# Output projection with a weight pool of its own and a two-part sample tile; up-projection weights on another queue

## The chip, the core and the metric

The kernel runs on one core of a Trainium2 chip. A core has a matrix engine (TensorE, PE in the rows, with its weight loads as PEld), three engines for elementwise work (VectorE as DVE, ScalarE as ACT, GpSimd as POOL), a queue engine (SyncE, SP) that here does nothing but issue transfers, and 16 DMA engines. ACT issues transfers too, in the order of its own instructions. Every engine runs its instructions in the order in which they were written down for it. The metric is device microseconds from the start to the end of one execution, as a median over executions.

## What is computed

One layer step for 1024 prompt tokens and 64 sample tokens, in float32. A normalised input goes through one input projection; its columns feed 8 heads of differential attention (A) and 16 heads of RWKV-7 time mixing (B); both outputs are gated, put side by side and sent through one output projection, whose normalised result is added to the input. Cut to what matters:

```python
h = rms_norm(x, norm_pre)
proj = h @ w_in
y_a = diff_attention(proj[q, k, v]) * silu(proj[g_a])
m = ps + (prev - ps) * mu_shift                  # token shift, ps = the B columns of proj
w_log = -softplus(-(w0 + tanh(wd) @ w_up)) - 0.5 # wd, ad: 64 columns of m each
a = sigmoid(a0 + ad @ a_up)
y_b = wkv_scan(r, exp(-exp(w_log)), k, v, a)     # then group norm, bonus, gate
mix = concat([y_a, y_b])                         # 2048 wide
out = mix @ w_out                                # 2048 x 1024
x_new = x + rms_norm(out, norm_post)
```

The outputs are x_new for prompt and sample, the keys and values, the final WKV states and the last shifted rows.

## The kernel before

**One program, several streams.** Python generators stand for streams of work. A planner (`Weave`) holds them by rank, keeps a clock of its own, and lets the stream of lowest rank that is ready write down its next instructions; a `yield` gives the modelled time after which a stream may go on, or a condition that it waits for. Streams of high rank are therefore filler: they go on where all others wait. A scheduler then sets each engine's order from this, with the semaphores and the waits for buffers. A pool hands out its tiles by tag, with `bufs` buffers for each tag; a tile that has no free buffer makes the instruction wait that writes it.

**Split operands.** A float32 operand is used as two parts of a format that TensorE takes: `hi` is a copy (ACT, L157) and `lo` the difference (POOL, L158). A product of two split operands takes three matmuls, hi x hi, lo x hi and hi x lo, added up in PSUM.

**Phase B** (`phase_b`) holds 17 units of the RWKV part (8 pairs of heads, two halves of the prompt each, and one unit for the sample, next to last, `p is None`). A unit begins with the up-projections (`w_up`, `a_up`): 64 x 128 weights of one pair, loaded twice, into both halves of a tile of pool tag `t` (5 buffers of 512 columns, `t512`), then split. `load_up` (L513) issues four transfers by ACT's queue (L519), one unit ahead by `next_up` in the unit before; the sample's unit loads four pairs, does their split and matmuls (L550 to L561), and then the other four, in place. Behind that come elementwise work, an inverse in six steps, and a chain over 8 chunks of 64 tokens (`sd` L869, `cbank` L862 to L890, `suv` L900). Filler is `filler` (rank 100): input projections by jobs of 128 columns (L226 to L228), with weights loaded by SP (L165) into a tile that the split of an earlier job has to free (L174).

**Phase A** (`phase_a`) holds the attention, 8 heads of 9 query tiles: `prep` loads a head's queries and keys by SP (`qa`, `ka`) and splits them, `score` and `qtile` do the scores (L1414, L1415), the softmax, and the product with the values (L1475); after four tiles they are turned (L1499) and stored to a DRAM tile `mixd`. Filler is what the projections have left, and then `out_projection`, which is entered when all projections are through and `hctx`, the memory of the projections, is closed; its pool `op` takes that memory.

**The output projection** goes over 7 groups of weights. Groups 0 to 5 are four 128-row blocks of `w_out` by one half (512 columns) of the output; the last has four blocks and both halves. Each group goes over 9 tiles of tokens, `tt` 0 to 7 for the prompt and 8 for the sample's 64. `load_wo` loads and splits a group's weights, into slots 0 to 3, 4 to 7 or 8 to 11, one group ahead; `load_mix` loads four blocks of `mixd` for a tile by SP (L1178) and splits them, for the sample after a memset of the whole tile (L1176), since 64 of its columns have no token. A job then takes for each block three matmuls of 512 columns into PSUM (`po`, two buffers, L1236 to L1238), and adds them to `part[tt]` on DVE (L1247), or copies them there on ACT in groups 0 and 2. In the last group `half_done` squares each half on ACT (L1206), and `finish` scales it by the norm, adds x and stores it (L1213 to L1225); for tiles 3 and 8 a quarter of that is done by POOL. The last group's order is 4, 5, 6, 7, 0, 1, 2, 3, 8, as the last head's query tiles come in the order 7 down to 0, and 8 behind them.

Of the kernel before, what the change touches and what calls it, by code (L numbers as in the profile page):

```python
# [11 lines left out]
F32 = mybir.dt.float32  # L12
# [293 lines left out]
def phase_b(tc, I, O, E):  # L306
# [8 lines left out]
    with ExitStack() as bs:  # L315
# [206 lines left out]
        def unit(n, p, hf):  # L522
# [19 lines left out]
            ups = [nxt.pop()] if nxt else []  # L542
            pss2 = yield from ps512(f"up{u}", 2)
            for q0 in range(0, 8, 4) if smp else (0,):
                if smp:
                    ups = [load_up(q) for q in range(q0, q0 + 4)]
                    yield W_DMA
                for i, raw in enumerate(ups):
                    ups[i] = t = t512(dt=F32R, nm=f"wus{u}{q0 + i}").rearrange("p (s c) -> p s c", c=P)
                    nc.scalar.copy(t[:, 0:2], raw[:, 0:2])  # L550
                    op_(ACT, 256)
                    gtt(t[:, 2:4], raw[:, 0:2], t[:, 0:2].bitcast(F32), op=SUB)
                    d = op_(POOL, 256)
                yield d
                for q, t in enumerate(ups):
                    for j, x in enumerate((xw, xa)):
                        o_ = pss2[j][:, (q0 + q) * CH:(q0 + q + 1) * CH] if smp else pss2[j]
                        cl = slice(TP, T) if smp else slice(hf * HALF, (hf + 1) * HALF)

                        mm(o_, t[:, j], x[:, cl], start=True, stop=False)  # L560
                        mm(o_, t[:, 2 + j], x[:, cl], start=False, stop=True)  # L561
# [487 lines left out]
        def filler():  # L1049
# [46 lines left out]
            yield lambda: len(roped) == 4 and b_done[0]  # L1096
# [18 lines left out]
def out_projection(tc, I, O, E):  # L1115
# [24 lines left out]
    jobs = [(g, tt) for g in range(7) for tt in ((4, 5, 6, 7, 0, 1, 2, 3, 8) if g == LAST else range(9))]  # L1140
# [436 lines left out]
```

## Time and profile before

| | us |
|---|---|
| median of 3 executions | 1816.07 |
| lowest, highest | 1812.95, 1818.63 |
| the profiled execution | 1819.35 |
| its span, first to last instruction | 1817.6 |
| PE busy in the span | 1678.9 |
| DVE, ACT, POOL busy | 1248.0, 846.4, 716.0 |

The profile is one execution. An engine's busy time counts its computing instructions and not the issue of transfers, so an ACT that issues looks idle. A row of a timeline gives start, duration, engine, line, operation and tiles; in brackets stands the idle time before it and what ended that. The granted clock of TensorE has two levels, 1.2 and 2.4 GHz; a stretch gives its mean as a share of the higher one. The row of a stretch gives, after its length, the busy time and in brackets the instructions of PE, PEld, DVE, ACT and POOL in this order.

### The profile page before, as it was taken

Reading aid. Unit: us, or ns where it says so; the run is one execution under the profiler, and the core shown is the slowest. Engines: PE = TensorE matmul, PEld = TensorE weight load, DVE = VectorE, ACT = ScalarE, POOL = GpSimd, SP = SyncE. Lnnn points to the kernel's source line nnn. Section 1 sums busy time; section 2 is a strip of 40 time slices with the busy share of each in tenths; the row PEclk is TensorE's granted clock in tenths of the full one; section 3 lists DMA queues with packets and bytes.
Section 4 is the critical chain, followed back from the end, with each engine's and each line's share of the span. In section 5 each row is a group of like instructions: output and inputs, shape, how many; then the busy total and the mean of one; then the engine's idle time right before and its main releaser. Section 6 shows DMA issues by size and latency. Waiting matters only on the chain.

```text
span 1817.6 us, 34309 instructions
## 1 busy us (share of the span) xinstructions
PE 1678.9 (92%) x12930; PEld 1500.6 (83%) x12930; DVE 1248.0 (69%) x2606; ACT 846.4 (47%) x2027; POOL 716.0 (39%) x901
## 2 busy tenths in 40 slices
PE   7999998999989989999999889989998898988997
PEld 5988888888878988898889888989887777777875
DVE  5667777678677778778777577744566476676736
ACT  6433443434433543444354344233556675665532
POOL 3433322332322433333342333112444757666563
PEclk9999999999999999999999899999999999999999
DMA  4210222221131111111111111436546455554345
GB/s 154 65 45 27 73 71 65 59 69 29 30 103 50 37 57 33 42 46 29 45 48 43 55 56 57 125 100 178 158 110 190 123 153 167 154 142 114 94 131 165
DMA packets 204096, 158.82 MB, mean 87 GB/s; under 512 B 44085, under 2 KB 185050, under 8 KB 203930
## 3 DMA queue, kind: packets, MB, share of 16 engines
q1 hardware_dynamic: 169098, 137.33, 26.3%
q10 hardware_dynamic: 34832, 19.30, 4.1%
q8 instruction: 102, 1.67, 0.4%
q14 instruction: 64, 0.52, 0.1%
HBM read 108.67 MB, written 47.34 MB: 86 GB/s over the span
## 4 chain that ended last, share of the span: by engine, by line
PE 56%; DVE 19%; POOL 7%; DMA 6%; issue 5%; ACT 5%; ACTq 1%; SPq 1%; POOLq 0%; DVEq 0%
PE x_o L1475 2%; PE po L1236 2%; PE po L1237 2%; PE po L1238 2%; PE cbank L890 2%; PE cbank L862 2%; PE s L1414 2%; PE m_s L689 2%; PE s L1415 1%; PE pj_g L226 1%; PE cbank L879 1%; PE pj_aq L226 1%; PE pj_av L226 1%; PE pj_g L227 1%; PE pj_k L226 1%
## 5 line engine op out<-in xcount | busy, mean ns | idle before, releaser
L869 ACT ACTIVATE sd<-suv,dc 64x64 f32<-64x64 f32 x128 | 44.4, 347 | 179.0 <-DVE suv L900 150.9
L1236 PE MATMUL po<-woh,mxh 128*128 128x512 f32 x288 | 122.1, 424 | 1.5 <-DVE part L1247 0.9
L1237 PE MATMUL po<-woh,mxl 128*128 128x512 f32 x288 | 115.7, 402 | 1.5 <-POOL mxl L158 1.5
L1238 PE MATMUL po<-wol,mxh 128*128 128x512 f32 x288 | 115.3, 400 | 1.8 <-POOL wol L158 1.8
L1431 ACT ACTIVATE e<-s,nb 128x128 f32<-128x128 f32 (+7 forms) x144 | 101.1, 708 | 33.5 <-DVE nb L1424 20.4
L158 POOL TENSOR_TENSOR mxl<-mxr,mxh 128x512 fp32r<-128x512 f32 x63 | 89.0, 1414 | 55.4 <-ACT mxh L157 53.0
L1475 PE MATMUL x_o<-vn,wt 128*128 128x128 f32 (+1 forms) x608 | 87.3, 289 | 11.8 <-DVE wt L1469 3.7
L1475 PEld LDWEIGHTS x_o<-vn,wt 128*128 128x128 f32 (+1 forms) x608 | 80.5, 200 | 21.0 <-DVE wt L1465 5.1
L1424 DVE TENSOR_REDUCE nb<-s 128x1 f32<-128x640 f32 (+8 forms) x104 | 95.5, 921 | 1.9
L735 POOL TENSOR_TENSOR ltlo<-lt,lt 64x512 f16<-64x512 f32 x32 | 37.6, 1173 | 129.4 <-ACT lt L723 128.2
L1414 PE MATMUL s<-k,qs 128*128 128x512 f32 (+4 forms) x208 | 76.6, 376 | 11.3 <-ACT e L1431 9.3
L900 DVE SCALAR_TENSOR_TENSOR suv<-cbank,dc,sd 64x64 f32<-64x64 f32 x224 | 63.1, 282 | 28.6 <-PE cbank L890 23.5
L890 PE MATMUL cbank<-suv,bkt 128*128 128x128 f32 x256 | 56.3, 302 | 24.5 <-DVE suv L886 24.3
L1415 PE MATMUL s<-k,qs 128*128 128x512 f32 (+4 forms) x208 | 71.2, 360 | 3.1 <-POOL k L1344 2.1
L226 PE MATMUL pj_k<-hhi,wh_k 128*128 128x384 f32 (+1 forms) x192 | 70.1, 365 | 1.9 <-ACT raw_k L241 1.9
L226 PE MATMUL pj_aq<-hhi,wh_aq 128*128 128x384 f32 (+1 forms) x192 | 71.5, 372 | 0.0
L226 PE MATMUL pj_av<-hhi,wh_av 128*128 128x384 f32 (+1 forms) x192 | 68.8, 358 | 2.5 <-DVE fl_g L999 2.1
L890 PEld LDWEIGHTS cbank<-suv,bkt 128*128 128x128 f32 x256 | 41.2, 189 | 36.0 <-DVE suv L886 33.9
L226 PE MATMUL pj_g<-hhi,wh_g 128*128 128x384 f32 (+1 forms) x192 | 70.6, 368 | 0.0
L226 PE MATMUL pj_ak<-hhi,wh_ak 128*128 128x384 f32 (+1 forms) x192 | 70.2, 365 | 0.0
L1247 DVE TENSOR_TENSOR part<-po,part 128x512 f32<-128x512 f32 x54 | 37.0, 686 | 47.7 <-PE po L1238 47.5
L226 PE MATMUL pj_v<-hhi,wh_v 128*128 128x384 f32 (+1 forms) x192 | 69.5, 362 | 0.0
(529 smaller groups left out, 6024.9 us busy)
## 6 DMA issues: line engine op xcount, KB each, us to landing
mxr<-mixB SPq DMA_DIRECT2D x32, 256.0 KB
wor<-in_w_out SPq DMA_DIRECT2D x64, 128.0 KB
qa<-scr_q SPq DMA_DIRECT2D x32, 204.0 KB
ka<-scr_k SPq DMA_DIRECT2D x32, 204.0 KB
mxr<-mixA SPq DMA_DIRECT2D x24, 256.0 KB
scr_q<-fl_q SPq DMA_DIRECT2D x8, 544.0 KB
scr_k<-fl_k SPq DMA_DIRECT2D x8, 544.0 KB
scr_v<-fl_v SPq DMA_DIRECT2D x8, 544.0 KB
```

Of the source, the lines that this page charges most:

```text
L158: gtt(lo, raw, hi.bitcast(F32), op=SUB)
L226: mm(ps[:, :n], hi[:, k, :], hhi[i][:, k, :], start=(k == 0), stop=False)
L890: mm(s, bkt[:, c], suv[:, c], start=True, stop=True)
L900: stt(suv[r, c + 1, h, :] if c < 7 and not smp else to[r], s[r, h * CH:(h + 1) * CH], dc[r, c:c + 1], sd[r], op0=MUL, op1=ADD)
L1236: mm(ps, hi[:, q, :], wh, start=(q == 0), stop=False)
L1237: mm(ps, lo[:, q, :], wh, start=False, stop=False)
L1238: mm(ps, hi[:, q, :], wl, start=False, stop=(q == len(ks) - 1))
L1414: mm(s2[:, b:b + w], lq, k1[c][:, k0 + o_:k0 + o_ + w], start=True, stop=False)
L1415: mm(s2[:, b:b + w], lq, k2[c][:, k0 + o_:k0 + o_ + w], start=False, stop=True)
L1424: nc.vector.tensor_reduce(nb[:, 0:m], s3[:, :, 0:n], axis=AX.X, op=MAX, negate=True)
L1431: act(e[:, 0:n], s3[:, j, 0:n], AF.Exp, bias=nb[:, j:j + 1], accum_out=st["sm"][:, c:c + 1])
L1475: mm(ops[:, 0:P], wt[0:w, b, :], vn[0:w, vb, :], start=(b == 0), stop=(b == len(kbs) - 1))
```

## The change

There are five edits.

1. The up-projection weights are loaded by SP's queue. The sample's unit takes them in four steps of four pairs of one matrix (512 columns, two transfers), the first loaded in the unit before, each further one a step ahead; each step has one split of 512 columns and eight matmuls of 64.
2. The four weight tiles of group 0 are loaded and split in phase A by a stream `first_wo` of rank 99.3, into a pool `wo0` that the slots 0 to 3 of all groups use from then on; the raw tile is one of the attention's (`kt`). The output projection is entered when they are there.
3. The sample's tile holds hi in columns 0 to 63 and lo in columns 64 to 127 of one operand; the matmul with lo and the memset are gone. Rows 64 to 127 of `part[8]` are then the products of lo, and in the last group they are brought to rows 0 to 63 by a transfer inside SBUF (`low`) and added on DVE before the norm.
4. The last group's order is 4, 5, 6, 7, 8, 0, 1, 2, 3, and the last head's query tile 8 comes behind tile 4.
5. In `finish`, everything is cut to the tile's rows, and the quarter on POOL is done for tiles 2 and 3.

```diff
         def next_up(n):
-            if n < len(order) and order[n][0] is not None:
-                nxt.append(load_up(order[n][0]))
+            if n < len(order):
+                nxt.append(load_up4(0, 0) if order[n][0] is None else load_up(order[n][0]))
...
-                    nc.scalar.dma_start(out=t[r:r + 64, s, :], in_=I[nm][0, :, q * P:(q + 1) * P])
+                    nc.sync.dma_start(out=t[r:r + 64, s, :], in_=I[nm][0, :, q * P:(q + 1) * P])
+            return t
+
+        def load_up4(q0, j):
+
+            t = t512(nm=f"wup4{q0}{j}")
+            for r in (0, 64):
+                nc.sync.dma_start(out=t[r:r + 64], in_=I[("w_up", "a_up")[j]][0, :, q0 * P:(q0 + 4) * P])
             return t
...
-            ups = [nxt.pop()] if nxt else []
+            raw = nxt.pop()
             pss2 = yield from ps512(f"up{u}", 2)
-            for q0 in range(0, 8, 4) if smp else (0,):
-                if smp:
-                    ups = [load_up(q) for q in range(q0, q0 + 4)]
+
+            if smp:
+                steps = [(q0, j) for q0 in (0, 4) for j in (0, 1)]
+                for i, (q0, j) in enumerate(steps):
+                    ahead = load_up4(*steps[i + 1]) if i < 3 else None
+                    hi = t512(dt=F32R, nm=f"wuh{u}{i}")
+                    lo = t512(dt=F32R, nm=f"wul{u}{i}")
+                    nc.scalar.copy(hi, raw)
+                    op_(ACT, 512)
+                    gtt(lo, raw, hi.bitcast(F32), op=SUB)
+                    yield op_(POOL, 512)
+                    for q in range(4):
+                        o_ = pss2[j][:, (q0 + q) * CH:(q0 + q + 1) * CH]
+                        mm(o_, hi[:, q * P:(q + 1) * P], (xw, xa)[j][:, TP:T], start=True, stop=False)
+                        mm(o_, lo[:, q * P:(q + 1) * P], (xw, xa)[j][:, TP:T], start=False, stop=True)
+                    spend(1200)
+                    raw = ahead
                     yield W_DMA
...
-            yield lambda: len(roped) == 4 and b_done[0]
+            yield lambda: len(roped) == 4 and b_done[0] and len(E["ws0"]) == 4
             E["hctx"].close()
...
-    jobs = [(g, tt) for g in range(7) for tt in ((4, 5, 6, 7, 0, 1, 2, 3, 8) if g == LAST else range(9))]
+    jobs = [(g, tt) for g in range(7) for tt in ((4, 5, 6, 7, 8, 0, 1, 2, 3) if g == LAST else range(9))]
...
+    wo0 = E["wo0"]
+    ws[0] = E["ws0"]
...
-            hi = op.tile([P, 512], F32R, tag=f"woh{t}", name=f"woh{k}{ch}")
-            lo = op.tile([P, 512], F32R, tag=f"wol{t}", name=f"wol{k}{ch}")
+            pool = wo0 if t < 4 else op
+            hi = pool.tile([P, 512], F32R, tag=f"woh{t}", name=f"woh{k}{ch}")
+            lo = pool.tile([P, 512], F32R, tag=f"wol{t}", name=f"wol{k}{ch}")
...
-        raw = op.tile([P, 4, P], F32, tag="mxr", bufs=2, name=f"mxr{g}{tt}")[:, 0:m]
-        if n < P:
-            nc.gpsimd.memset(raw, 0.0)
+        raw = op.tile([P, 4, P], F32, tag="mxr", bufs=2, name=f"mxr{g}{tt}")[:, 0:m, 0:n]
...
-        lo = op.tile([P, 4, P], F32R, tag="mxl", bufs=MB, name=f"mxl{g}{tt}")[:, 0:m]
-        yield split_op(hi, lo, raw, m * P)
+        if n < P:
+
+            lo = None
+            yield split_op(hi[:, :, 0:n], hi[:, :, n:], raw, m * n)
+        else:
+            lo = op.tile([P, 4, P], F32R, tag="mxl", bufs=MB, name=f"mxl{g}{tt}")[:, 0:m]
+            yield split_op(hi, lo, raw, m * P)
...
-            if q % 9 == 0 and g < LAST:
+            if q % 9 == 0 and 0 < g < LAST:
...
     def half_done(tt, ch):
 
+        if tt == 8:
+
+            if ch == 0:
+                return
+            low = op.tile([P, D], F32, tag="x", bufs=2, name="low")[0:TS]
+            nc.sync.dma_start(out=low, in_=part[8][TS:P])
+            vtt(part[8][0:TS], part[8][0:TS], low, op=ADD)
+            half(tt, 0)
+        half(tt, ch)
...
-        m = 768 if tt in (3, 8) else D
+        m = 768 if tt in (2, 3) else D
...
-                mm(ps, lo[:, q, :], wh, start=False, stop=False)
+                if lo is not None:
+                    mm(ps, lo[:, q, :], wh, start=False, stop=False)
...
+    E["wo0"] = wo0 = E["ctx"].enter_context(tc.tile_pool(name="wo0", bufs=1))
+    E["ws0"] = {}
+
+    def first_wo():
+        for i, k in enumerate(range(8, 12)):
+            yield 8000
+            raw = ap_.tile([P, HALF], F32, tag="kt", name=f"wo0r{k}")
+            nc.sync.dma_start(out=raw, in_=I["w_out"][0, k * P:(k + 1) * P, 0:512])
+            yield W_DMA
+            hi = wo0.tile([P, 512], F32R, tag=f"woh{i}", name=f"woh{k}0")
+            lo = wo0.tile([P, 512], F32R, tag=f"wol{i}", name=f"wol{k}0")
+            split(hi, lo, raw)
+            op_(ACT, 512)
+            yield op_(POOL, 512)
+            E["ws0"][k, 0] = hi, lo
+    weave.add(99.3, first_wo())
...
-        for o_, qt in enumerate((0, 1, 8, 2, 3, 4, 5, 6, 7) if h < 7 else (7, 6, 5, 4, 3, 2, 1, 0, 8)):
+        for o_, qt in enumerate((0, 1, 8, 2, 3, 4, 5, 6, 7) if h < 7 else (7, 6, 5, 4, 8, 3, 2, 1, 0)):
```

## Rows read from the trace of the kernel before

**Rows 1.** Page, parts 1 and 4: busy time; the chain's shares by engine.

```profile
PE 1678.9 (92%) x12930; PEld 1500.6 (83%) x12930; DVE 1248.0 (69%) x2606; ACT 846.4 (47%) x2027; POOL 716.0 (39%) x901
...
PE 56%; DVE 19%; POOL 7%; DMA 6%; issue 5%; ACT 5%; ACTq 1%; SPq 1%; POOLq 0%; DVEq 0%
```

**Rows 2.** Stretches: from:to, length, busy (instructions), PE's clock, DMA share, GB/s.

```profile
800.00:1000.00 200.00, 195.28 (x1738) 179.64 (x1737) 156.18 (x349) 90.50 (x205) 69.95 (x82) 1.00 0.14 42
1757.00:1807.00 50.00, 49.06 (x215) 39.68 (x213) 32.89 (x42) 16.84 (x42) 16.61 (x18) 1.00 0.52 172
```

**Rows 3.** Timeline of PE where attention ends: start, duration, what, count.

```profile
1726.59 0.27 PE L1499 MATMUL x_z<-ident,on 128*128 128x128 f32 x1
```

**Rows 4.** Tile mxr: count, ns least/median/most, first and last start.

```profile
L158 POOL TENSOR_TENSOR mxl<-mxr,mxh x63: 1262/1291/2450, 1401.3 to 1791.4; 128x512 fp32r<-128x512 f32 x63
...
L1176 POOL MEMSET mxr<- x7: 525/527/529, 1450.9 to 1782.1; 128x512 f32 x7
```

**Rows 5.** Timeline of PE, from the projections to the output projection.

```profile
1388.28 0.31 PE L228 MATMUL pj_ag<-hhi,wl_ag 128*128 128x320 f32 x1
...
1407.88 0.77 PE L1236 MATMUL po<-woh,mxh 128*128 128x512 f32 x1
...
1431.03 0.50 PE L1238 MATMUL po<-wol,mxh 128*128 128x512 f32 x1 [1.47 <-POOL wol L158]
```

**Rows 6.** Stretches there, and the one behind.

```profile
1385.00:1408.00 23.00, 15.09 (x92) 12.28 (x90) 12.40 (x32) 13.19 (x41) 10.30 (x13) 0.86 0.70 228
1408.00:1435.00 27.00, 23.20 (x129) 18.23 (x128) 19.77 (x34) 18.18 (x47) 16.57 (x24) 0.93 0.53 142
1435.00:1460.00 25.00, 23.73 (x140) 20.20 (x138) 7.52 (x18) 15.33 (x42) 20.93 (x24) 1.00 0.46 122
```

**Rows 7.** Timelines of ACT and POOL there: the first mixed tile's split.

```profile
1400.62 0.62 ACT L157 CAST mxh<-mxr 128x512 fp32r<-128x512 f32 x1 [4.69 <-DMA mxr<-mixB]
...
1401.32 1.27 POOL L158 TENSOR_TENSOR mxl<-mxr,mxh 128x512 fp32r<-128x512 f32 x1 [10.03 <-ACT mxh L157]
```

**Rows 8.** DMA in the stretch from 1395 to 1408: its total.

```profile
DMA packets 3896, 3.95 MB, mean 304 GB/s; under 512 B 241, under 2 KB 3313, under 8 KB 3896
```

**Rows 9.** The stretch in which the attention's first head is loaded.

```profile
1255.00:1280.00 25.00, 20.82 (x122) 19.01 (x120) 6.52 (x13) 9.19 (x18) 5.73 (x3) 0.91 0.87 221
```

**Rows 10.** Timeline of ACT: issues of up loads, their casts, and sd.

```profile
72.39 2.03 ACTq L519 DMA_DIRECT2D t_wup<-in_a_up  x2
...
81.35 0.39 ACT L550 CAST t_wus<-t_wup 128x256 fp32r<-128x256 f32 x1
...
309.02 0.47 ACTq L519 DMA_DIRECT2D t_wup<-in_a_up  x1
...
335.00 0.41 ACT L550 CAST t_wus<-t_wup 128x256 fp32r<-128x256 f32 x1
...
1016.99 1.80 ACTq L519 DMA_DIRECT2D t_wup<-in_w_up  x2
...
1028.03 0.35 ACT L869 ACTIVATE sd<-suv,dc 64x64 f32<-64x64 f32 x1 [10.78 <-DMA t_wup<-in_w_up]
```

**Rows 11.** Timeline of PE behind the sixteen issues.

```profile
1029.06 0.49 PE L890 MATMUL cbank<-suv,bkt 128*128 128x128 f32 x2 [3.65 <-DVE suv L886]
```

**Rows 12.** Stretches there, before and with the wait.

```profile
1005.00:1025.00 20.00, 19.62 (x177) 18.24 (x176) 12.22 (x31) 5.64 (x15) 6.58 (x7) 1.00 0.25 78
1025.00:1041.00 16.00, 11.88 (x88) 10.81 (x88) 6.66 (x14) 5.16 (x12) 3.94 (x5) 0.68 0.05 15
```

**Rows 13.** Waits of ACT on up loads: total us, times, longest us.

```profile
ACT sd L869 <- DMA t_wup<-in_w_up: 19.7, 3, 10.8
```

**Rows 14.** Timeline of DVE in the last group: the finish's add.

```profile
1766.43 1.22 DVE L1220 TENSOR_TENSOR part<-part,fx 128x1024 f32<-128x1024 f32 x1
```

**Rows 15.** Waits of SP's queue, one kind: total us, times, longest us.

```profile
SPq L165 <- POOL wl_v L174: 118.0, 15, 20.1
```

**Rows 16.** Timeline of PE: a wait inside the attention.

```profile
1611.14 1.05 PE L1475 MATMUL x_o<-vn,wt 128*128 128x128 f32 x7 [2.77 <-DVE wt L1465]
```

More of the change, by code (lines that the diff above doesn't have):

```diff
@@ L541, in unit @@
                 next_up(0)
-            ups = [nxt.pop()] if nxt else []
+            raw = nxt.pop()
             pss2 = yield from ps512(f"up{u}", 2)
-            for q0 in range(0, 8, 4) if smp else (0,):
-                if smp:
-                    ups = [load_up(q) for q in range(q0, q0 + 4)]
-                    yield W_DMA
[L548 to L561, printed above, removed]
+            if smp:
[14 more added lines that the diff above has]
+                    raw = ahead
+                    yield W_DMA
+            else:
+                t = t512(dt=F32R, nm=f"wus{u}").rearrange("p (s c) -> p s c", c=P)
+                nc.scalar.copy(t[:, 0:2], raw[:, 0:2])
+                op_(ACT, 256)
+                gtt(t[:, 2:4], raw[:, 0:2], t[:, 0:2].bitcast(F32), op=SUB)
+                yield op_(POOL, 256)
+                for j, x in enumerate((xw, xa)):
+                    cl = slice(hf * HALF, (hf + 1) * HALF)
+                    mm(pss2[j], t[:, j], x[:, cl], start=True, stop=False)
+                    mm(pss2[j], t[:, 2 + j], x[:, cl], start=False, stop=True)
@@ L1173, in load_mix @@
         src = mixd["A" if ks[0] < 8 else "B", j]
-        raw = op.tile([P, 4, P], F32, tag="mxr", bufs=2, name=f"mxr{g}{tt}")[:, 0:m]
-        if n < P:
-            nc.gpsimd.memset(raw, 0.0)
+        raw = op.tile([P, 4, P], F32, tag="mxr", bufs=2, name=f"mxr{g}{tt}")[:, 0:m, 0:n]
         r0 = (ks[0] % 8) * P
-        nc.sync.dma_start(out=raw[:, :, 0:n], in_=src[r0:r0 + m * P, o_ * P:o_ * P + n].rearrange(
+        nc.sync.dma_start(out=raw, in_=src[r0:r0 + m * P, o_ * P:o_ * P + n].rearrange(
             "(k c) t -> c k t", c=P))
@@ L1181, in load_mix @@
         hi = op.tile([P, 4, P], F32R, tag="mxh", bufs=MB, name=f"mxh{g}{tt}")[:, 0:m]
[L1182 to L1183 removed]
+        if n < P:
+            lo = None
+            yield split_op(hi[:, :, 0:n], hi[:, :, n:], raw, m * n)
+        else:
+            lo = op.tile([P, 4, P], F32R, tag="mxl", bufs=MB, name=f"mxl{g}{tt}")[:, 0:m]
+            yield split_op(hi, lo, raw, m * P)
         mix[q] = hi, lo
@@ L1199, in half_done, with half @@
     def half_done(tt, ch):
+        if tt == 8:
[6 more added lines that the diff above has]
+        half(tt, ch)
+    def half(tt, ch):
+        n = P if tt < 8 else TS
         if ch == 0:
             x_ = op.tile([P, D], F32, tag="x", bufs=2, name=f"fx{tt}")
-            nc.scalar.dma_start(out=x_[:P if tt < 8 else TS], in_=x_rows(tt))
+            nc.scalar.dma_start(out=x_[:n], in_=x_rows(tt))
             fin[tt] = x_, op.tile([P, 2], F32, tag="ms", bufs=2, name=f"fm{tt}")
         sq = op.tile([P, 512], BF16, tag="sq", name=f"fs{tt}{ch}")
-        act(sq, part[tt][:, ch * 512:(ch + 1) * 512], AF.Square, accum_out=fin[tt][1][:, ch:ch + 1])
+        act(sq[:n], part[tt][:n, ch * 512:(ch + 1) * 512], AF.Square, accum_out=fin[tt][1][:n, ch:ch + 1])
     def finish(tt):
@@ L1236, in out_projection @@
                 mm(ps, hi[:, q, :], wh, start=(q == 0), stop=False)
-                mm(ps, lo[:, q, :], wh, start=False, stop=False)
+                if lo is not None:
+                    mm(ps, lo[:, q, :], wh, start=False, stop=False)
                 mm(ps, hi[:, q, :], wl, start=False, stop=(q == len(ks) - 1))
-                spend(690)
+                spend(690 if lo is not None else 460)
                 if q < len(ks) - 1:
@@ L1260, in phase_a @@
     nh, ident, hsl = (E[k] for k in ("nh", "ident", "hsl"))
-    scr, mixd, mixed, weave = (E[k] for k in ("scr", "mixd", "mixed", "weave"))
+    scr, mixd, mixed, weave, split = (E[k] for k in ("scr", "mixd", "mixed", "weave", "split"))
     projected, roped = E["projected"], E["roped"]
```

13 lines of the change are left out of this document (7 added, 6 removed).

## The prediction

> **What bounds the kernel now.** I read the page's first table, then the shares of the chain that ended last, then busy time by stretch. TensorE is busy 92% of the span, no other engine that computes over 69%, and 56% of the chain runs through PE, 19% through DVE [rows 1]. By stretch, the reader is to look at length minus PE busy: 4.7 us idle in the 200 from 800 on, 0.9 us in the last 50 that hold matmuls, 1757 to 1807 [rows 2]. One queue of filler (input projections, then the output projection) stands behind the latency-bound chains, and it lasts to the end: the last attention output is turned at 1726.59 [rows 3], so the 80 us from there to 1807 are output projection alone. The time is then PE's work, plus PE's idle time, plus what the lower clock costs. Matmuls removed anywhere, or idle time closed anywhere, should shorten the end by their own length, since the filler moves up.
>
> **Matmuls of the sample's tile (L1236 to L1238).** Before, each (k, column half) of tile 8 takes three 512-column matmuls, after two: the operand carries hi in its columns 0 to 63 and lo in 64 to 127, so one pass against the weights' hi part gives both products. Groups 0 to 5 have 4 such steps, the last group 8: 32 matmuls go. Matmuls overlap, so what one costs is the pitch: 215 started in 49.06 us of PE busy, 0.228 us each [rows 2]. 32 x 0.228 = **7.3 us less**. As many weight loads go, which lie beside the matmuls. POOL loses seven memsets of 0.53 us and half of seven splits of 1.29 us [rows 4], 8 us over a stretch of 400 on an engine that is no bound: I take nothing, at best 2 us.
>
> **The first weights of the output projection.** Before, they can be loaded only when the projections' memory is closed. The last projection matmul starts at 1388.28, the first po matmul at 1407.88, and then the stream is throttled by weights, as at 1431.03, where it waits for wol [rows 5]. What is lost from 1385 to 1435: idle 7.9 + 3.8 = 11.7 us, and clock 0.86 over 23 us and 0.93 over 27, which is 3.2 + 1.9 = 5.1 us of full speed, together 16.8 us; the stretch behind loses 1.3 us in 25, so 2.6 in 50 [rows 6]. **At most 14 us** can come back. Not all does: the first mixed tile is still loaded after the close, ACT stands 4.69 us on its DMA and its lo part is ready at 1402.6 [rows 7]; nothing shortens that, and the second group's weights are now loaded at that moment in place of the first's, so DMA stays as full (304 GB/s [rows 8]). What early weights save is 1402.6 to 1407.9, 5.3 us, at a lower clock and partly filled by attention (some 3 us of it), and about half of the 3.8 us of idle behind. I take **5 us less**, bounds 0 and 12. The four early loads stand on SP at the start of the attention phase; each brings ACT a split of 0.62 us [rows 7] and POOL one of 1.29 us [rows 4], as it did later. They fall to 1255 to 1300, where DMA is 0.87 busy and PE idles 4.2 us in 25 [rows 9]; the first head's loads, casts and splits stand behind them on SP, ACT and POOL, and PE's first scores behind those. I take **1 us more**, bounds 0 and 4 (two of these loads and splits in front of the head). The raw tile is shared with a head's key output; a clash there is inside these bounds.
>
> **Up-projection weights.** Before, ScalarE's queue issues 96 small loads. For the sample's second half sixteen stand in a row from 1016.99, and ACT's next operation, an sd of the other unit's chain, starts at 1028.03 after 10.78 us [rows 10]; PE idles 3.65 us for that chain [rows 11]. Loss from 1025 to 1041: 4.1 us idle and 16 x 0.32 = 5.1 us of clock, 9.2 us, against 0.4 us in the 20 us before [rows 12]. After, the sample has eight loads in place of 32, on SP, each asked for one step ahead, so ACT isn't held; but its four steps in a row, each with a split of 512 elements, have to pass ACT and POOL, and live on the five tiles of their pool. I take **6 us less**, bounds 0 and 9. For the other 16 units, four issues each of some 0.6 us, 38 us of ACT's queue, go to SP [rows 10]. ACT waited behind such issues three times, 19.7 us with the 10.78 [rows 13]; the other two make 8.9 us, and no idle of PE over 0.9 us stands near them: **1 us less**, bounds 0 and 4. SP's own cost for 72 issues is small; what stands ahead of them in its queue is the risk, below.
>
> The skill has a rule against this part. The Trainium skill, page "DMA: Bandwidth & Descriptors", section "Issuing engines are not separate DMA queues", says that loads from several issuers run on the same 16 DMA engines, and that the choice of issuer saves only the time to initiate, "which is usually small relative to the DMA itself". By it the 7 us above would be near nothing. The row shows sixteen issues that hold ACT for 10.78 us, so the sum goes by the row, and the rule stays as a rival.
>
> **The sample's last step and the end.** Tile 8 moves from last to fifth of nine in the last group, and needs its lower 64 rows added to the upper: one DMA inside SBUF, through SP, and a DVE add that waits for it. Behind that add on DVE stand the evacuations of po, for which PE waits after two tiles. DVE idles 17.1 us of the last 50 [rows 2], an add of a full tile takes 1.22 us [rows 14], and the wait for the DMA is bounded by the 4.69 us of a load in the fullest stretch [rows 7]: **1 us more**, bounds 0 and 5. Last is now a tile of 128 rows, 512 KB out in place of 256; at 304 GB/s [rows 8] that is **0.8 us more**, bounds 0 and 2. The finish shared by two engines stands at the last two tiles before and after.
>
> **Sum:** -7.3 - 5 + 1 - 6 - 1 + 1 + 0.8 = -16.5 us. The profiled execution took 1819.35 us, 1817.6 of it span; it would become 1802.9. It lay 3.3 us above the median of 1816.07; from there 1799.6, and I say **1800**. With all bounds one way it is 1816.07 - 7.3 - 2 - 12 - 9 - 4 = 1782, the other way 1816.07 - 7.3 + 4 + 5 + 2 = 1820. All at their ends together is unlikely; the forecast's own band is 1788 to 1810. Each edit also changes the order that is written down for all engines, which no row prices; the band allows for it.
>
> **Rivals.**
> (a) Up weights late: **slower**. SP waits in order, up to 20.1 us at a time until a weight tile comes free [rows 15]. An up load written behind such a wait comes late, and PE stands at that unit's first matmul. For it: a short lead, 7 us between the last issue, over at 74.4, and the cast at 81.35. Against it: a usual lead of 25 us (309.5 to 335.0) [rows 10], longer than the longest wait. It decides from the point where the wait exceeds the lead less the load's own time. At 2 us of PE in each of 16 units that is 32 us, with -7.3 - 5 + 2.8 beside it and nothing gained on ACT: 1816.07 + 22.5 = **1838**.
> (b) The gain is given back: **no change**. If attention's own waits set the length up to 1727 and the filler only lies beside it, then only matmuls behind that point count: the 8 of the last group and perhaps 4 more, some 2.5 us; idle closed earlier opens as a wait of the same chains later. For it: PE idles between 1465 and 1675 that wait for ACT or DVE, as the 2.77 us at 1611.14 [rows 16]. Against: 80 us of pure filler remain behind. 1816.07 - 2.5 = **1813**.
> (c) The change doesn't do what it says on ACT: the sample's stall is that unit's own chain, where ACT and POOL take turns, the issue time was hidden, and the 7 us don't come: -9.5, **1807**. It is also what the skill's rule would make of it.
>
> **Chances.** Forecast 0.58; (c) 0.15; (b) 0.14; (a) 0.07; a gain beyond the band, from a luckier order, 0.06. About 0.3%, 5.4 us, is what a measurement of this kernel can tell from no change, so faster is below 1810.6 and slower above 1821.5. Forecast, beyond and most of (c) are faster: 0.78. Same: (b) and the rest of (c), 0.14. Slower: (a) and a little of the forecast's own costs, 0.08. The range that leaves out no more than 0.2 is 1788 to 1814: it drops (a), the gain beyond, and a part of (b).
>
> **What would show it.** Right: 32 fewer po matmuls; no wait of ACT that ends in the issue of an up load, PE dense and at the full clock around the sample's up matmuls; the first po matmul within some 14 us of the last projection matmul and no wait for wol behind it; the stretch between the last attention matmul and the last po matmul as dense as before. Wrong: PE's m_up matmuls waiting for a split whose load SP issued late (a); the same total of PE idle under other names (b); PE idle around the sample with nothing issued on ACT (c); PE idle behind the add of tile 8.

## The result, and the profile after

| | before | after |
|---|---|---|
| median, us (4 executions each, side by side) | 1816.43 | 1792.76 |
| lowest, highest | 1812.95, 1818.63 | 1790.80, 1793.45 |
| the profiled execution, its span | 1819.35, 1817.6 | 1792.56, 1790.8 |

The ratio is 0.987 (95%: 0.9852 to 0.9887), 23.7 us less. Measured a second time, the changed kernel had a median of 1794.68 and a ratio of 0.989 (0.9862 to 0.9918); one of its six executions there took 1858.08 us at a mean granted clock of 0.843, and is left out of both. Forecast was 1800, 1788 to 1814: direction, range and most mechanisms held; the sum of 16.5 was too small.

The page of the changed kernel, parts 1, 4 and 5 (the last: count | busy, mean ns | idle ahead and what ended most of it):

```profile
PE 1662.0 (93%) x12898; PEld 1485.1 (83%) x12898; DVE 1246.3 (70%) x2607; ACT 842.1 (47%) x2019; POOL 705.7 (39%) x886
...
PE 57%; DVE 19%; POOL 7%; issue 5%; DMA 5%; ACT 5%; ACTq 0%; SPq 0%; POOLq 0%; DVEq 0%
...
L1273 PE MATMUL po<-woh,mxh 128*128 128x512 f32 x288 | 122.9, 427 | 7.0 <-DVE part L1285 4.8
...
L1276 PE MATMUL po<-wol,mxh 128*128 128x512 f32 x288 | 116.3, 404 | 1.4 <-POOL wol L158 1.4
...
L1275 PE MATMUL po<-woh,mxl 128*128 128x512 f32 x256 | 104.1, 407 | 2.3 <-POOL mxl L158 2.3
```

PE has 32 matmuls fewer than in [rows 1], all of them in the line with `mxl`. The chain is as it was: what bounds the kernel hasn't changed. The span is 26.8 us shorter, of which PE's busy time makes 16.9 and its idle time 9.9. The next paragraphs show where it went, by stretches that end at the same work. `m_ib` is a group of four transposes in each unit of phase B; here are those of the unit ahead of the sample's and of the one behind, on PE's timeline, before:

```profile
956.83 0.60 PE L618 MATMUL m_ib<-ident,t_inx 128*128 128x128 f32 x4
...
1102.13 0.60 PE L618 MATMUL m_ib<-ident,t_inx 128*128 128x128 f32 x4
```

and after:

```profile
957.37 0.60 PE L635 MATMUL m_ib<-ident,t_inx 128*128 128x128 f32 x4
...
1091.03 0.60 PE L635 MATMUL m_ib<-ident,t_inx 128*128 128x128 f32 x4
```

**The sample's unit**: 145.30 us became 133.66. Up to it nothing had come in (956.83 and 957.37). The stretch itself, before and then after:

```profile
958.00:1102.00 144.00, 132.07 (x1138) 120.80 (x1137) 98.11 (x216) 56.54 (x131) 47.28 (x51) 0.94 0.19 56
```

```profile
958.50:1091.00 132.50, 126.04 (x1150) 115.94 (x1150) 96.94 (x218) 55.64 (x127) 45.64 (x47) 1.00 0.21 61
```

Idle fell from 11.9 to 6.5 us, and the granted clock rose from 0.94 to 1.00, so that 12 matmuls more take 6 us less of PE's busy time.

**The transition** (against [rows 5 to 7]), PE, then ACT, then the stretch:

```profile
1387.76 0.50 PE L1273 MATMUL po<-woh,mxh 128*128 128x512 f32 x1 [2.18 <-ACT mxh L157]
```

```profile
1387.09 0.62 ACT L157 CAST mxh<-mxr 128x512 fp32r<-128x512 f32 x1 [2.59 <-DMA mxr<-mixB]
```

```profile
1375.60:1415.00 39.40, 32.55 (x182) 25.41 (x180) 26.75 (x58) 24.35 (x68) 13.46 (x20) 0.96 0.66 189
```

From the last projection matmul (1375.60) to the first po matmul 12.16 us pass, after 19.60. The first po matmul now waits for the mixed tile alone. From the last projection matmul to the last turn of attention (x_z) 338.31 became 326.54; that single traces differ in this stretch without edit 2 too is shown below, at h_early.

**The tail** gave something back. PE stands for POOL before the last turn, which runs at the lower clock (0.52 from 1702 to 1707), and twice for DVE in the last group. The kernel before has no such wait for POOL at its last turns, and for DVE in the last group none over 0.70 us:

```profile
1702.14 1.11 PE L1555 MATMUL x_z<-ident,on 128*128 128x128 f32 x4 [5.88 <-POOL on L1548]
...
1755.51 0.47 PE L1273 MATMUL po<-woh,mxh 128*128 128x512 f32 x1 [1.49 <-DVE part L1285]
...
1771.82 0.79 PE L1273 MATMUL po<-woh,mxh 128*128 128x512 f32 x1 [2.24 <-DVE part L1285]
```

From the last turn to the end it is 88.7 us after 91.0, though 31 fewer po matmuls lie there (some 7 us).

### The profile page after: what moved, and what is told of

Same layout as the page of the kernel before. It is cut to its first block, busy times and chain, and to the rows that moved or that the text cites. A ratio compares the mean times of both kernels' runs of the same rounds, so it can differ in the third digit from the quotient of the medians.

```text
span 1790.8 us, 34215 instructions
## 1 busy us (share of the span) xinstructions
PE 1662.0 (93%) x12898; PEld 1485.1 (83%) x12898; DVE 1246.3 (70%) x2607; ACT 842.1 (47%) x2019; POOL 705.7 (39%) x886
## 4 chain that ended last, share of the span: by engine, by line
PE 57%; DVE 19%; POOL 7%; issue 5%; DMA 5%; ACT 5%; ACTq 0%; SPq 0%; POOLq 0%; DVEq 0%
PE x_o L1531 3%; PE po L1273 2%; PE po L1276 2%; PE po L1275 2%; PE cbank L907 2%; PE m_s L706 2%; PE cbank L879 2%; PE s L1470 1%; PE x_wt L1517 1%; PE cbank L896 1%; PE s L1471 1%; PE pj_g L226 1%; PE pj_k L226 1%; PE pj_av L226 1%; PE pj_av L228 1%
## 5 line engine op out<-in xcount | busy, mean ns | idle before, releaser
L1487 ACT ACTIVATE e<-s,nb 128x256 f32<-128x256 f32 (+8 forms) x144 | 100.9, 706 | 30.4 <-DVE nb L1480 22.9
L1275 PE MATMUL po<-woh,mxl 128*128 128x512 f32 x256 | 104.1, 407 | 2.3 <-POOL mxl L158 2.3
L158 POOL TENSOR_TENSOR mxl<-mxr,mxh 128x512 fp32r<-128x512 f32 x56 | 75.6, 1351 | 75.3 <-ACT mxh L157 75.2
L1531 PEld LDWEIGHTS x_o<-vn,wt 128*128 128x128 f32 (+1 forms) x608 | 79.3, 197 | 10.1 <-DVE wt L1521 2.7
L1470 PE MATMUL s<-k,qs 128*128 128x512 f32 (+4 forms) x208 | 74.1, 366 | 2.2 <-ACT e L1487 1.7
L1471 PE MATMUL s<-k,qs 128*128 128x512 f32 (+4 forms) x208 | 69.0, 350 | 4.0 <-POOL k L1400 2.3
L1273 PEld LDWEIGHTS po<-woh,mxh 128*128 128x128 f32 x288 | 55.8, 194 | 18.9 <-ACT mxh L157 4.5
L226 PE MATMUL pj_r<-hhi,wh_r 128*128 128x384 f32 (+1 forms) x192 | 68.7, 358 | 0.0
```

Of the source, the lines that this page charges most:

```text
L158: gtt(lo, raw, hi.bitcast(F32), op=SUB)
L226: mm(ps[:, :n], hi[:, k, :], hhi[i][:, k, :], start=(k == 0), stop=False)
L1273: mm(ps, hi[:, q, :], wh, start=(q == 0), stop=False)
L1275: mm(ps, lo[:, q, :], wh, start=False, stop=False)
L1470: mm(s2[:, b:b + w], lq, k1[c][:, k0 + o_:k0 + o_ + w], start=True, stop=False)
L1471: mm(s2[:, b:b + w], lq, k2[c][:, k0 + o_:k0 + o_ + w], start=False, stop=True)
```

## The experiments

Twelve runs followed the first, each timed beside the kernel before. The last column is the ratio's distance from 1 on 1816.4 us. The changed kernel's own executions lie up to 14 us apart (1790.8 to 1804.9; what differs between them is in the last section), so single traces are compared here by stretches, and totals by their intervals.

| kernel | median | ratio (95%) | us against before |
|---|---|---|---|
| after, first time | 1792.76 | 0.987 (0.9852 to 0.9887) | -23.6 |
| after_again | 1794.68 | 0.989 (0.9862 to 0.9918) | -20.0 |
| e_up_before: after without edit 1 | 1806.62 | 0.9944 (0.9924 to 0.9965) | -10.2 |
| e_late_first: after without edit 2 | 1808.66 | 0.9955 (0.9937 to 0.9973) | -8.2 |
| e_three: after without edit 3 | 1798.44 | 0.989 (0.9865 to 0.9914) | -20.0 |
| e_order: after without 4, POOL's quarter for 3 and 8 | 1796.94 | 0.9882 (0.9858 to 0.9905) | -21.4 |
| e_issuer: after, issued by ACT | 1795.68 | 0.9875 (0.9854 to 0.9897) | -22.7 |
| f_issuer: before, issued by SP | 1808.84 | 0.9957 (0.9938 to 0.9977) | -7.8 |
| h_early: before with edit 2 | 1812.99 | 0.9983 (0.9969 to 0.9996) | -3.1 |
| h_two: before with edits 3 to 5 | 1815.49 | 1.0006 (0.9988 to 1.0024) | +1.1 |
| g_wol_turn: after, tail varied | 1801.62 | 0.9915 (0.9892 to 0.9937) | -15.4 |
| g_last31: after, last weights earlier | 1802.61 | 0.9935 (0.9912 to 0.9958) | -11.8 |
| g_last31_turn: the same, turn later | 1800.99 | 0.9928 (0.9901 to 0.9954) | -13.1 |

**The changed kernel again.** No edit.

> The changed kernel itself once more, beside the next three: 1793 (1790 to 1797). It gives the scatter against which the single edits are read.

The median of 1794.68 is as expected, but the five executions spread from 1791.5 to 1804.9, wider than the range. It is the measure for the three kernels timed beside it (e_issuer, f_issuer, g_wol_turn).

**Edit 1, undone, and in halves.** e_up_before has the old form on ACT's queue:

```diff
-                nxt.append(load_up4(0, 0) if order[n][0] is None else load_up(order[n][0]))
+            if n < len(order) and order[n][0] is not None:
+                nxt.append(load_up(order[n][0]))
...
-                    ahead = load_up4(*steps[i + 1]) if i < 3 else None
+                    ups = [load_up(q) for q in range(q0, q0 + 4)]
```

> The changed kernel, with the up-projection weights as they were before the change: 96 small loads by ACT's queue, the sample's unit with four pairs loaded in place, twice. All else as in the changed kernel (1792.8). Theory as the two traces read: from 958 to the second unit behind the sample the change saved 15.0 us (idle 3.8 plus clock, before 132.07 busy in 144 at 0.94, after 126.04 in 132.5 at 1.00), nearly all of it by this part, and the filler carries it to the end: 1807 (1804 to 1810). The sizes of the prediction for this part (6 for the sample and 1 for the other units): 1800. Rival, the issue time was hidden and the saving came from another edit or a luckier order: 1793 (within 2).

Measured 1806.62, as the first theory said. The stretch between the two `m_ib` is 144.97 us, as before:

```profile
956.68 0.60 PE L618 MATMUL m_ib<-ident,t_inx 128*128 128x128 f32 x4
...
1101.65 0.60 PE L618 MATMUL m_ib<-ident,t_inx 128*128 128x128 f32 x4
```

e_issuer keeps the new form and gives it back to ACT:

```diff
-                nc.sync.dma_start(out=t[r:r + 64], in_=I[("w_up", "a_up")[j]][0, :, q0 * P:(q0 + 4) * P])
+                nc.scalar.dma_start(out=t[r:r + 64], in_=I[("w_up", "a_up")[j]][0, :, q0 * P:(q0 + 4) * P])
```

(and the same in `load_up`).

> The changed kernel with one thing undone: the up-projection weights are issued by ACT's queue again, in the new form (the sample's eight loads of 512 columns, one step ahead; four small loads for each of the other units). Theory one, what counted is that sixteen issues stood in a row ahead of ACT's next work: now two stand ahead of a step, 1.3 us, and four ahead of a unit, 2.4 us, so nearly all stays gained: 1794 (1792 to 1797). Theory two, any issue on ACT costs the chains: the other units' three waits come back too, 1800 or more. Theory three, the issuer's load beside SP's long waits cost something and ACT is better: 1790 or less.

1795.68: nothing is lost that can be told, as theory one said. Its timeline on PE, then on ACT (ACTq is an issue):

```profile
960.26 0.60 PE L635 MATMUL m_ib<-ident,t_inx 128*128 128x128 f32 x4
...
1093.93 0.60 PE L635 MATMUL m_ib<-ident,t_inx 128*128 128x128 f32 x4
```

```profile
1010.45 0.47 ACTq L526 DMA_DIRECT2D t_wup<-in_w_up  x1
...
1013.53 0.47 ACTq L526 DMA_DIRECT2D t_wup<-in_w_up  x1
...
1015.69 1.23 ACTq L526 DMA_DIRECT2D t_wup<-in_a_up  x2
```

133.67 us, the same as with SP (133.66). The issues are there, but no more than two of those shown stand in a row ahead of ACT's next work. f_issuer is the other half, the old form with the 96 small loads on SP:

```diff
-                    nc.scalar.dma_start(out=t[r:r + 64, s, :], in_=I[nm][0, :, q * P:(q + 1) * P])
+                    nc.sync.dma_start(out=t[r:r + 64, s, :], in_=I[nm][0, :, q * P:(q + 1) * P])
```

> The kernel before with one thing changed: the 96 small loads of up-projection weights go to SP's queue; the sample's unit still loads four pairs at a time in place. Theory one, ACT held for 10.78 us by sixteen issues is what cost: the stretch from 1017 to 1102, which lost 20.2 us to idle and clock, loses 8 or less, and the whole is 1804 (1801 to 1808). Theory two, the stall is the unit's own chain of load, cast and split in place, and who issues is indifferent: 1816 (1813 to 1819), with the same idle around the sample.

```profile
957.33 0.60 PE L618 MATMUL m_ib<-ident,t_inx 128*128 128x128 f32 x4
...
1094.55 0.60 PE L618 MATMUL m_ib<-ident,t_inx 128*128 128x128 f32 x4
```

137.22 us and 7.8 us in all (4.2 to 11.3), against theory two, though the median is just above the range of theory one, and the stretch loses more than the 8 us that it allowed: from 1017 to 1095 PE idles 8.2 us at a mean clock of 0.96. ACT isn't held: the `sd` that stood behind the issues follows the chain's own step on DVE. Its row here, then that step in the kernel before:

```profile
1020.64 0.35 ACT L869 ACTIVATE sd<-suv,dc 64x64 f32<-64x64 f32 x1 [4.88 <-DVE suv L900]
```

```profile
1019.85 0.60 DVE L900 SCALAR_TENSOR_TENSOR suv<-cbank,dc,sd 64x64 f32<-64x64 f32 x2 [1.06 <-PE cbank L890]
```

There the step was done at 1020.4 and the `sd` started at 1028.03 [rows 10]: the issues held it for 7.6 us, and the first 3 of the 10.78 would have been idle in any case. Either half takes most of the stall, because either takes the sixteen issues in a row off ACT; the new form does 3.6 us better than the old form on SP. Behind the stretch of [rows 12] the kernel before loses more, to a second wait of PE, for DVE. f_issuer keeps that wait; the changed kernel doesn't have it. First the stretch and the wait before, then the wait in f_issuer:

```profile
1041.00:1060.00 19.00, 14.49 (x127) 12.77 (x127) 12.56 (x23) 7.69 (x18) 8.50 (x10) 0.83 0.20 53
```

```profile
1047.18 0.64 PE L752 MATMUL m_iq<-xt,q 64*64 64x64 f16 x16 [3.19 <-DVE q L746]
```

```profile
1039.62 0.44 PE L752 MATMUL m_iq<-xt,q 64*64 64x64 f16 x16 [3.17 <-DVE q L746]
```

Between the two `m_ib` the nine traces with the new form have 133.64 to 133.74 us, the four with the old form on ACT 144.81 to 145.49: this reading doesn't hang on the scatter.

**Edit 2, undone and alone.** e_late_first, after without the early stream and its pool:

```diff
-    weave.add(99.3, first_wo())
...
-            pool = wo0 if t < 4 else op
-            hi = pool.tile([P, 512], F32R, tag=f"woh{t}", name=f"woh{k}{ch}")
+            hi = op.tile([P, 512], F32R, tag=f"woh{t}", name=f"woh{k}{ch}")
...
-            if q % 9 == 0 and 0 < g < LAST:
+            if q % 9 == 0 and g < LAST:
```

> The changed kernel, with the first group's weights loaded where they were before, when the projections' memory is closed; no stream of early loads, no pool of their own. All else as in the changed kernel (1792.8). Theory as the traces read: the distance from the last projection matmul to the first of the output projection was 19.6 us and is 12.2, and it comes back, with idle behind it for wol; the whole stretch from there to the last attention matmul had shortened by 11.8 us: 1801 (1798 to 1804). The sizes of the prediction (5 saved, 1 paid for the early loads): 1797. Rival, attention's own work fills that stretch and the gain came from the order alone: 1793 (within 2), with the same total of idle elsewhere.

1808.66, more than even the theory said, and the place is another. The first po matmul comes 13.80 us behind the last projection matmul, nearly as early as with edit 2 (12.16). The loss that its trace shows lies behind it, where PE waits for weights, group after group (its timeline of PE):

```profile
1393.47 0.80 PE L1273 MATMUL po<-wol,mxh 128*128 128x512 f32 x1 [1.77 <-POOL wol L158]
...
1421.40 0.79 PE L1273 MATMUL po<-wol,mxh 128*128 128x512 f32 x1 [3.50 <-POOL wol L158]
...
1542.29 0.69 PE L1273 MATMUL po<-wol,mxh 128*128 128x512 f32 x1 [4.03 <-POOL wol L158]
...
1602.31 0.50 PE L1273 MATMUL po<-wol,mxh 128*128 128x512 f32 x1 [3.14 <-POOL wol L158]
```

12.4 us; the changed kernel has one such wait there:

```profile
1582.49 0.50 PE L1276 MATMUL po<-wol,mxh 128*128 128x512 f32 x1 [1.45 <-POOL wol L158]
```

From the last projection matmul to the last turn it is 334.2 us and not 326.5, with 36.6 us of idle and not 29.7. The trace is of the fastest of the twelve executions (1801.92), so it shows some 8 of the 12 to 15 us that the ratios give (-8.2 against -20.0 and -23.6); where the rest lies isn't shown. h_early is edit 2 on the kernel before:

```diff
+    weave.add(99.3, first_wo())
...
+    ws[0] = E["ws0"]
...
-            if q % 9 == 0 and g < LAST:
+            if q % 9 == 0 and 0 < g < LAST:
```

> The kernel before with edit 2 alone: the first group's weights are loaded and split early in the attention phase, into a pool of their own. Theory, as the run without that part reads: the loads of every later group then start without the first group's in front of them, the waits of PE for wol behind the last projection go, and the stretch from the last projection matmul to the last turn of attention, 338.3 before, is near 327 as in all runs that have the part: 1804 (1801 to 1808). The size of the prediction (5 saved, 1 paid): 1812. Rival, it needs the other edits to bring anything, since attention's own waits set that stretch in the order of before: 1815 or more.

1812.99: 3.1 us less (0.7 to 5.6), the size of the prediction and not that of the theory, which fell: from the last projection matmul to the last turn it has 334.6 us and not 327. Nor does that stretch measure edit 2 alone. f_issuer, which has none of edits 2 to 5, takes 329.94 us for it, where the kernel before takes 338.31:

```profile
1380.03 0.31 PE L228 MATMUL pj_ag<-hhi,wl_ag 128*128 128x320 f32 x1
...
1709.97 0.27 PE L1499 MATMUL x_z<-ident,on 128*128 128x128 f32 x1
```

So how much of the 11.8 us there is edit 2's can't be read from two traces; what it is worth is read from the ratios. The kernel before has few waits for weights to lose there: at 1.47 us [rows 5] the only one over 0.8.

**Edit 3, undone; edits 3 to 5 alone; edit 4 undone.** e_three leaves the order of the changed kernel:

```diff
+        if n < P:
+            nc.gpsimd.memset(raw, 0.0)
...
-                if lo is not None:
-                    mm(ps, lo[:, q, :], wh, start=False, stop=False)
+                mm(ps, lo[:, q, :], wh, start=False, stop=False)
...
```

> The changed kernel, with the sample's tile by three matmuls for each block and half, on a memset and two operands as before the change; the order of the tiles stays as in the changed kernel, and the transfer and the add that bring the lower rows up are gone. Theory, 32 matmuls at a pitch of 0.228: 7.3 more, less some 2 to 3 for the waits around that transfer and add: 1797.5 (1796 to 1800). Rival, the last stretch holds waits that more filler would only fill (the last tile behind attention waits 5.9 us for POOL, and PE then runs 4.5 us at half clock): 1793 (within 2).

1798.44, in the range of the theory; but by the ratios that is only 0 to 3.6 us behind the changed kernel, and not to be told from after_again. Its trace has neither the 5.88 nor the two waits for DVE: it has 32 matmuls more and three waits less. h_two, the edits on the kernel before:

```diff
-    jobs = [(g, tt) for g in range(7) for tt in ((4, 5, 6, 7, 0, 1, 2, 3, 8) if g == LAST else range(9))]
+    jobs = [(g, tt) for g in range(7) for tt in ((4, 5, 6, 7, 8, 0, 1, 2, 3) if g == LAST else range(9))]
...
-                mm(ps, lo[:, q, :], wh, start=False, stop=False)
+                if lo is not None:
+                    mm(ps, lo[:, q, :], wh, start=False, stop=False)
```

> The kernel before with edits 3 to 5 alone: the sample's tile with both parts in one operand, the order of the last group and of the last head, the quarter on POOL for tiles 2 and 3. Theory one, 32 matmuls at 0.228 come off the end but for some 2 us for the transfer and the add: 1811 (1809 to 1813). Theory two, the last stretch gives nearly all of it back, since the last turn of attention then waits for POOL's splits of the last weights: 1815 (1813 to 1818), with that wait in the trace.

1815.49: no gain, as theory two said, but the wait that it named isn't in the trace. PE's timeline has weights again, not the last turn:

```profile
1431.88 0.50 PE L1255 MATMUL po<-wol,mxh 128*128 128x512 f32 x1 [1.47 <-POOL wol L158]
...
1546.59 0.50 PE L1255 MATMUL po<-wol,mxh 128*128 128x512 f32 x1 [0.99 <-POOL wol L158]
...
1551.38 0.50 PE L1255 MATMUL po<-wol,mxh 128*128 128x512 f32 x1 [2.15 <-POOL wol L158]
...
1614.19 0.80 PE L1255 MATMUL po<-wol,mxh 128*128 128x512 f32 x1 [6.11 <-POOL wol L158]
```

The last three are 9.3 us that the kernel before doesn't have, more than the 7.3 of the matmuls. Yet PE's idle time from the last projection matmul to the last turn is 34.3 us after 35.2: other waits of the same chains are shorter. That the waits for weights are why the matmuls bring nothing is therefore likely and not shown. e_order takes the orders of before and keeps the operand in two parts:

```diff
-    jobs = [(g, tt) for g in range(7) for tt in ((4, 5, 6, 7, 8, 0, 1, 2, 3) if g == LAST else range(9))]
+    jobs = [(g, tt) for g in range(7) for tt in ((4, 5, 6, 7, 0, 1, 2, 3, 8) if g == LAST else range(9))]
...
-        m = 768 if tt in (2, 3) else D
+        m = 768 if tt in (3, 8) else D
...
-        for o_, qt in enumerate((0, 1, 8, 2, 3, 4, 5, 6, 7) if h < 7 else (7, 6, 5, 4, 8, 3, 2, 1, 0)):
+        for o_, qt in enumerate((0, 1, 8, 2, 3, 4, 5, 6, 7) if h < 7 else (7, 6, 5, 4, 3, 2, 1, 0, 8)):
```

> The changed kernel, with the orders of before: in the last head the query tile of the sample is last, and in the last group of the output projection its tile is last; the quarter on POOL for tiles 3 and 8. The operand in two parts stays, so the transfer and the add that bring the lower rows up now stand at the very end, with PE through. Theory one, the wait of 5.9 us before the last turn of attention, with 4.5 us of half clock behind it, comes from the new order: it goes, and the end pays some 3 us for the transfer and the add: 1789 (1787 to 1791). Theory two, that wait comes from the splits of the last group's weights, which fall there in any order, and the end pays in full: 1796 (1794 to 1798).

1796.94, no difference that can be told. Its timeline of SP's queue and DVE shows what the order spares: with tile 8 last, the transfer and the add stand bare behind PE's last matmul, and from its start to the end of the span it is 15.1 us and not 9.3.

```profile
1780.52 0.49 SPq L1230 DMA_DIRECT2D low<-part  x1
...
1783.55 1.22 DVE L1231 TENSOR_TENSOR part<-part,low 64x1024 f32<-64x1024 f32 x1 [2.19 <-DMA low<-part]
```

What it has instead of the changed kernel's 5.88 are 3.94 and 0.97 us for POOL at the last turns, against theory one, and no wait for DVE over 0.7 us in the last group.

**The tail.** POOL's rows in the changed kernel, behind the last matmul ahead of the 5.88:

```profile
1695.03 1.29 POOL L158 TENSOR_TENSOR mxl<-mxr,mxh 128x512 fp32r<-128x512 f32 x1
1696.28 2.76 POOL L158 TENSOR_TENSOR wol<-wor,woh 128x256 fp32r<-128x256 f32 x4
1699.01 0.19 POOL L1545 TENSOR_SCALAR ms<-ms 128x1 f32<-128x1 f32 x1
...
1701.47 0.61 POOL L1548 TENSOR_SCALAR on<-on,ms 128x128 f32<-128x128 f32 x1
```

Two norms stand behind four splits of the last weights. Three kernels tried to have that back: g_wol_turn makes those splits on DVE and writes the last turn down later,

```diff
+                    vtt(lo[:, c0:c0 + 256], raw, hi[:, c0:c0 + 256].bitcast(F32), op=SUB)
+                    yield op_(DVE, 256)
...
-            yield d
+            yield d + (4000 if h == 7 and qt == 0 else 0)
```

> The changed kernel with two edits at its tail: the lo parts of the last group's weights are made by DVE and not POOL, and the last turn of attention is written down 4 us of the planner's time later, so that matmuls of the output projection stand ahead of it on PE. Theory, the 5.9 us that PE stood for POOL at the last turn, and the 2.2 us that the half clock behind it cost, can be had back: 1786 (1784 to 1789). Rival, the same wait appears at the next matmul, which needs the split of its own operand from POOL, or DVE is held in its place: 1793 (within 2).

g_last31 loads half of them 16 tiles earlier (31 in place of 47 in the loader's count; the expectation says 23), and g_last31_turn does that with the later turn:

```diff
+            elif q == 31:
+                weave.add(99.2, load_wo(LAST, 1))
```

> The changed kernel with one edit: the half of the last group's weights that has slots of its own (8 to 11) is loaded and split some 23 tiles earlier, and no longer beside the last turn of attention. Theory, POOL's splits of those weights are what the last turn waited for (5.9 us, and 2.2 us of clock behind it), and the matmuls taken out come off the end once the wait is gone: 1787 to 1791 where the changed kernel takes 1793 to 1798. Rival, the wait has another cause (that head's own chain on ACT and POOL) and stays: no difference.

> As the last, and the last turn of attention is written down 4 us of the planner's time later, so that matmuls of the output projection stand ahead of it. Theory: as the last or up to 2 us less, since PE has work ahead of the turn. Rival: those matmuls need a split from POOL too, and the wait only changes its name: as the last.

None is better, and g_last31 is slower than the changed kernel's first measurement. In g_wol_turn the wait moved: 3.23 us at the turn, and then

```profile
1710.01 0.79 PE L1279 MATMUL po<-woh,mxh 128*128 128x512 f32 x1 [7.80 <-ACT woh L157]
```

In g_last31 the turn still waits, and PE waits twice for weights where the changed kernel doesn't, 0.90 and 2.86 us (g_last31_turn has 2.27, 1.89, and 6.42 at the turn):

```profile
1644.97 0.74 PE L1287 MATMUL po<-wol,mxh 128*128 128x512 f32 x1 [2.86 <-POOL wol L158]
...
1712.36 1.11 PE L1566 MATMUL x_z<-ident,on 128*128 128x128 f32 x4 [6.41 <-POOL on L1559]
```

There POOL works without a gap from 1701.08 to the last norm, through two mixed tiles, six splits of the half that still comes late, and three norms. What was expected, that the splits of the other half made the wait, falls: the wait stands at POOL's queue as a whole, and nothing here got it back.

## Why the prediction was right, and where its sizes were off

- **Total.** 1800 against 1792.76 and 1794.68, inside 1788 to 1814. Edit 1 was put at -7, edits 2 to 5 at -9.5. Edits 2 to 5 without edit 1 measure -10.2 (-13.8 to -6.4), right as a sum; but alone edit 2 measures -3.1 and edits 3 to 5 +1.1, where the working has -4 and -5.5, so that the sum came out is partly luck. The missing size is edit 1's: undone, it costs 10 to 13 us.
- **The sample's up-projection, -6, bounds 0 and 9.** It measured -11.6, above its own bound. The mechanism held: with the issues off ACT and nothing else (f_issuer) the stretch is 8.1 us shorter, near the 9.2 that the working read from 1025 to 1041 [rows 12] and then cut to 6. What failed is the window: from 1041 to 1060 PE also idled 4.5 us and ran at 0.83. Of that, the wait of 3.19 us for DVE's `q` isn't the issues', since f_issuer keeps it; with the new form it is gone, and the stretch is 3.6 us shorter again. In all, from 958 to 1102 idle and clock (0.94) cost 11.9 and some 8 us, after 6.5 and nothing. Why the new form spares the second wait isn't shown (e_up_before and h_two, with the old form on ACT, don't have it either and take as long as before).
- **The other 16 units' issues, -1.** Nothing: the first and the last `m_ib` ahead of the sample lie 887.67 us apart before and 890.26 after, and e_issuer, with these issues on ACT, loses nothing that can be told. The working gave these units 8.9 us of ACT's waits [rows 13]; 3.77 of that, at 998.91, lie in the sample's unit.
- **Rival (c) and the rule of the Trainium skill.** The rival, that issue time was hidden, is refuted by f_issuer. The Trainium skill, page "DMA: Bandwidth & Descriptors", section "Issuing engines are not separate DMA queues", has DMAs started on several engines save only the time to initiate them, usually small: e_issuer agrees (133.67 us against 133.66); in f_issuer that time isn't small, since sixteen issues stood ahead of work that a chain waits for, for 7.6 us (145.30 to 137.22).
- **32 matmuls, -7.3.** The count is exact; the step that failed is the first part's general claim, that matmuls removed anywhere shorten the end by their length. Alone (h_two: +1.1 us, -2.2 to +4.4, where the working has -5.5 for edits 3 to 5) they bring nothing, which is rival (b)'s result: nearly the same total of PE's idle time under other names, here for the next group's weights. With the weights a group ahead they seem to count: 1806.62 with edits 2 to 5 against 1812.99 with edit 2, 6.4 us (by the ratios 7.1, give or take 4.5), though edits 4 and 5 are in that difference. In the changed kernel undoing edit 3 costs 0 to 3.6 us; its own tail waits 9.6 us at places where e_three doesn't.
- **First weights, -5 and +1.** Alone -3.1, near the -4. Undone from the changed kernel it costs 12 to 15. The working had seen that the second group's loads take the first's place, but not that later groups are then on time for a faster stream: 12.4 us of waits for weights without edit 2, 1.45 with it. The early loads cost nothing to be seen: from `shp`, the last transpose of phase B, to the first score 27.09 us pass, after 27.55.
- **The first mixed tile.** As forecast it sets the first po matmul; this was ready at 1387.7 at the earliest, 12 us behind the last projection matmul.
- **`low`, +1, and the last output, +0.8.** DVE waits 1.06 us for the transfer, and the two waits of PE for DVE in the last group make 3.7 us: within 0 to 5. The 4.69 us that served as the bound are ACT's idle time ahead of a load's landing [rows 7], not a load's time; here the add starts 5.3 us behind the issue (1757.78 to 1763.07). From the start of PE's last matmul to the end of the span it is 9.3 us after 11.0, so the larger output costs nothing beyond what the rest of the end gives.
- **Rival (a)**, up loads late on SP: no matmul of the up-projection stands in the list of PE's waits over 0.7 us.

**What stays open.** The single effects don't add up: edit 1 undone costs 10 to 13 us, edit 2 undone 12 to 15, alone edit 2 brings 3, and edits 3 to 5 bring nothing. That edit 2 and edits 3 to 5 bring more together (-10.2) than one by one (-2.0) is shown by the times, and the waits for weights in e_late_first and h_two suggest why; with f_issuer's stretch as short as it is, single traces don't show it. But e_three, which has edits 1, 2, 4 and 5, is as fast as all five together; edits 1 and 2 by themselves weren't run, so how much of the matmuls' 7.3 us is in the final 20 to 24 can't be said within the 4 us of these intervals.

## What to carry to other kernels

Sixteen transfers that an engine issued in a row ahead of its next link of a chain held that link back by 7.6 us, and taking them off gave 8.1 us, a spell of low clock included; spread out one step ahead, they cost nothing to be seen on either queue. Work removed from a filler stream need not shorten the end: the edits that took out 32 matmuls brought nothing alone and some 6 to 7 us on top of early weights, so price such edits together, and after each matmul taken out ask when the next weights are ready. And measure a stall from the last dense stretch ahead of it to the first dense one behind it, clock included.

## What the runs showed of the hardware

One program, instruction for instruction, took from 1790.8 to 1804.9 us. The first table of the profiled execution of after_again stands beside the one shown above:

```profile
PE 1672.1 (93%) x12898; PEld 1496.1 (83%) x12898; DVE 1246.3 (69%) x2607; ACT 842.4 (47%) x2019; POOL 705.3 (39%) x886
```

The same 12898 matmuls are busy 10.1 us longer, while DVE, ACT and POOL take the same; the mean granted clock is 0.980 and not 0.986, and the spans lie 12.2 us apart. Six us of it had come by 958, ahead of everything that the change's larger parts touch. TensorE was longer at its lower level of 1.2 GHz in one of the two. So single traces of this kernel can't settle a question of 5 us unless the stretch is one, as the sample's, that keeps its length.
